# The end of the last tile in a streaming encoder: loads of x on GpSimd's queue, the sample's tokens in four column groups

## The chip, the core and the metric

The kernel runs on one core of a Trainium2 chip. Its engines are TensorE (PE; weight loads are shown as PEld), VectorE (DVE), ScalarE (ACT), GpSimd (POOL) and SyncE (SP, which only issues transfers). The metric is device time in microseconds (us) of one launch; the median of three runs of the kernel before is 2172.12 us.

## What is computed

A two-layer encoder step for 1024 prompt tokens and 32 sample tokens that share all weights. Layer 0 mixes tokens with a spatial-gating unit, layer 1 with pooling windows; each is followed by a channel MLP, each with norms before and behind, and scales that come from a condition vector per group. What matters here is the last line of layer 1:

```python
f = jnp.square(jax.nn.relu(h @ ffn_w_up[i])) @ ffn_w_down[i]
x = x + gt2 * rmsnorm(f, g_norm[i, 3])      # y_prompt (1, 1024, 1024), y_sample (1, 32, 1024)
```

`rmsnorm` divides each token by the root of the mean square of its 1024 channels.

## The kernel before

Activations lie with channels on the 128 partitions (8 blocks of 128 channels, `KB`) and tokens along the columns. There are three tiles of tokens: 384, 384, and 256 prompt tokens with the 32 sample tokens behind them (288 columns). Every float32 matrix product is made of three products of split (high and low) parts. The MLP goes through its 4096 hidden channels in 8 chunks of 512; `ffn_item` does one chunk for one tile: four hidden blocks (`up`), then `down`, which for each of 8 output blocks `d` makes 12 products into one PSUM buffer (three of the kind `pd` rotate) and lets VectorE add them to the accumulator `acc`. Chunks 6 and 7 of layer 1 are done for the first two tiles together, and then for the last tile alone. Apart from a part at the start, the framework's scheduler decides the order on each engine; a helper only feeds it work in the program's order.

For the first two tiles the end (`to_out`, `run`) scales the result, adds x, transposes 32x32 blocks on VectorE (tile `turned`), and writes each channel block with four transfers of 48 KB, three by SP's queue and one by GpSimd's. For the last tile the end is taken apart so that little is left behind the last product:

- In `mix_to_ffn` the x that must be added at the end is written to a scratch tensor `xsd` in HBM.
- In `down`, in chunk 7, block by block: `st.square(d)` squares on ScalarE and sums over blocks on VectorE; `scale_last(d)` (line 1340) scales by a channel's coefficient on ScalarE; `turn_last` (line 1362) turns finished blocks by TensorE, so that tokens lie on partitions.
- `scale_last(0)` also issues the nine loads of x by SP: four of 32 partitions for each of two groups of 128 prompt tokens, one for the 32 sample tokens (`LAST`). Each is 1024 pieces of 128 bytes. VectorE transposes 32x32 blocks of them (line 1355) from `xlast_l` to `xlast_h`.
- `last` (line 1566) turns the rest, sums the squares over partitions by products with ones (`pn_last`, line 1574), takes the reciprocal root with one correction step, and for each of three groups (two of 128 tokens, one of 32) and each half of the channels does one multiply-add on VectorE, `x + r * y`, and one output transfer by SP (line 1602).

`LAST` takes the sample's 32 tokens as the lower rows of a full group of 128 columns, so the turned sample has 32 used partitions and 1024 columns. `room(part, t, name)` gives the buffer that held part `h` or `l` of tile `t`; `xlast_l` and `xlast_h` use those of tile 0.

The framework gives each transfer of SP and ScalarE one of eight landing semaphores, and each of GpSimd one of eight others.

Of the kernel before, what the change touches and what calls it, by code (L numbers as in the profile page):

```python
# [12 lines left out]
ALU = mybir.AluOpType  # L13
AX = mybir.AxisListType

P = 128
D = 1024
KB = D // P
SEQ = 1024
DEC = 32  # L20
# [6 lines left out]
TILES = [(0, 384, 0), (384, 384, 0), (768, 256, DEC)]  # L27
NT = len(TILES)
# [6 lines left out]
def tile_stream_encoder_step(  # L35
# [25 lines left out]
    nc = tc.nc  # L61
    act = nc.scalar.activation
    mm = nc.tensor.matmul
# [33 lines left out]
    ncol = [p + s for _, p, s in TILES]  # L97
# [20 lines left out]
    xd = [dram.tile([P, KB, n], F32, name=f"xd{t}") for t, n in enumerate(ncol)]  # L118
    vd = dram.tile([SEQ + DEC, SGU], F32, name="vd")

    LAST = [(0, 0, P), (P, 0, P), (ncol[-1] - P, P - DEC, DEC)]
    xsd = dram.tile([DEC, KB, P // DEC, ncol[-1]], F32, name="xsd")

    ident = const.tile([P, P], F32, name="ident")
# [21 lines left out]
    def A(t, kb, c0=0, w=None):  # L146
        w = ncol[t] - c0 if w is None else w
        return acc[t][:, kb, HALO + c0 : HALO + c0 + w]


    def room(part, t, name, dtype=F32):
        return work.tile([P, KB, ncol[t]], dtype, tag=f"h{part}{t}", bufs=1, name=name)
# [7 lines left out]
    def ps_ms(name):  # L160
        return psum.tile([P, 512], F32, tag="pm", bufs=3, name=name)
# [7 lines left out]
    def t_st(name):  # L169
        return small.tile([P, 4], F32, tag="st", bufs=6, name=name)  # L170
# [1112 lines left out]
    def ffn_item(p, t, after):  # L1283
        l, c, tiles = passes[p]
        last = t == tiles[-1]
        n = ncol[t]
        hid = []

        def up(j):
            ps = ps_up(f"pf{l}_{c}_{t}_{j}")  # L1290
            products(ps, n, up_terms(("up", p, j), t))
            if last:
                w_finish(("up", p, j))
            r = t_m(f"r{l}_{c}_{t}_{j}")
            act(out=r[:, :n], in_=ps[:, :n], func=AF.Relu)  # L1295
            a, b = t_hid("h", f"fh{l}_{c}_{t}_{j}"), t_hid("l", f"fl{l}_{c}_{t}_{j}")
            act(out=r[:, :n], in_=r[:, :n], func=AF.Square)
            split(a, b, r, n)
            hid.append((a, b))

        def down():
            for d in range(KB):
                ps = ps_dn(f"pg{l}_{c}_{t}_{d}")
                wh, wl = need_w(("dn", p, d // 2))
                terms = []
                for j in range(4):
                    o = j * 256 + (d % 2) * P
                    a, b = hid[j]
                    terms.append((wh[:, o : o + P], wl[:, o : o + P], a[:, :n], b[:, :n]))
                products(ps, n, terms)  # L1310
                accumulate(t, d, ps, c == 0)
                if d == 0 and after is not None:
                    st = Stat(t, f"rf{l}_{t}", l == 0 or t < NT - 1)
                if after is not None:
                    st.square(d)
                    if l == 1 and t == NT - 1:
                        scale_last(d)
                        if d in (2, 4, 6):
                            turn_last(d - 2)
                            turn_last(d - 1)  # L1320
                if last and d % 2 == 1:
                    w_finish(("dn", p, d // 2))
                weave(d % 2)
            if after is not None:
                after(st)

        for j in range(4):
            up(j)
            weave()
            if j == 0:  # L1330
                flush()
        pending.append(down)


    last_ps = {}

    def scale_last(d):
        t = NT - 1
        if d == 0:
            last_ps["x"], last_ps["raw"] = (  # L1340
                room(part, 0, f"xlast_{part}").rearrange("p k n -> p (k n)").rearrange(
                    "p (b d) -> p b d", d=D
                )
                for part in "hl"
            )
            src = xsd.rearrange("c k q n -> c (k q) n")
            for i, (c0, r0, nr) in enumerate(LAST):
                for r1 in range(r0, r0 + nr, DEC):
                    nc.sync.dma_start(
                        last_ps["raw"][r1 : r1 + DEC, i, :].rearrange("p (m n) -> p m n", n=DEC),  # L1350
                        src[:, :, c0 + r1 : c0 + r1 + DEC],
                    )
        if d in (3, 4, 5):
            i, r0, nr = d - 3, LAST[d - 3][1], LAST[d - 3][2]
            nc.vector.transpose(
                out=last_ps["x"][r0 : r0 + nr, i, :], in_=last_ps["raw"][r0 : r0 + nr, i, :]
            )
        for c0, w, v in segs[t]:
            a = A(t, d, c0, w)
            act(out=a, in_=a, func=AF.Copy, scale=coef[:, 1, 3, v, d : d + 1])  # L1360

    def turn_last(d):
        half = d // 4
        for i, (c0, _, _) in enumerate(LAST):
            if d % 4 == 0:
                take = ps_up if half == 0 and i < 2 else (ps_ms if half == 0 or i < 2 else ps_dn)
                last_ps[(i, half)] = take(f"yT{i}_{half}")
            nc.tensor.transpose(
                last_ps[(i, half)][:, (d % 4) * P : (d % 4 + 1) * P], A(NT - 1, d, c0, P), ident
            )  # L1370

    def mix_to_ffn(st, l):
        t = st.t
# [182 lines left out]
    def to_out(st):  # L1556
        t = st.t
        col0, npr, nsm = TILES[t]
        blocks = [
            (c * P, P, y_prompt[0, col0 + c * P : col0 + (c + 1) * P, :]) for c in range(npr // P)  # L1560
        ]
        if nsm:
            blocks.append((npr, nsm, y_sample[0]))

        def last():

            turn_last(KB - 2)
            pn = ps_dn("pn_last")
            nb = len(LAST)
            for k in (0, KB - 1):  # L1570
                if k > 0:
                    turn_last(KB - 1)
                for i, (c0, _, _) in enumerate(LAST):
                    mm(
                        pn[:, 2 * i : 2 * i + 2],
                        st.sq[:, k, c0 : c0 + P],
                        ones[:, 0:2],
                        start=k == 0 and i == 0,
                        stop=k > 0 and i == nb - 1,
                        skip_group_check=True,  # L1580
                    )
            sums = pn[:, : 2 * nb].rearrange("p (b c) -> p b c", c=2)[:, :, 0]
            r, q = (t_st(f"{x}_last")[:, :nb] for x in ("r", "q"))
            act(out=r, in_=sums, func=AF.Abs_reciprocal_sqrt, scale=1.0 / D)
            tt(out=q, in0=r, in1=r, op=ALU.mult)
            stt(out=q, in0=sums, scalar=-0.5 / D, in1=q, op0=ALU.mult, op1=ALU.mult)
            stt(out=r, in0=q, scalar=1.5, in1=r, op0=ALU.add, op1=ALU.mult)
            xt = last_ps["x"]
            dsts = [dst for _, _, dst in blocks]
            for i, (_, r0, nr) in enumerate(LAST):  # L1590
                rows = slice(r0, r0 + nr)
                for half in range(2):
                    d = slice(half * 512, half * 512 + 512)
                    stt(
                        out=xt[rows, i, d],
                        in0=last_ps[(i, half)][rows, :],
                        scalar=r[rows, i : i + 1],
                        in1=xt[rows, i, d],
                        op0=ALU.mult,
                        op1=ALU.add,  # L1600
                    )
                    nc.sync.dma_start(dsts[i][:, d], xt[rows, i, d])
            yield False

        def run():
            need_ada(1, 5)
            if t == NT - 1:
                yield from last()
                return
            yield from residual(st, 1, 3, f"r2_1_{t}", [], store=False, stat=False)  # L1610
            turned = room("h", t, f"turned{t}")
            dst = y_prompt[0, col0 : col0 + npr, :].rearrange(
                "(b i) (k q c) -> q k i b c", i=DEC, q=P // DEC, c=DEC
            )
            for k in range(KB):
                time["dve"] += 0.1 + npr / 930.0
                nc.vector.transpose(out=turned[:, k, :], in_=A(t, k))
                for q in range(P // DEC):
                    (nc.gpsimd if q == 3 else nc.sync).dma_start(
                        dst[q, k],  # L1620
                        turned[DEC * q : DEC * (q + 1), k, :].rearrange("p (b c) -> p b c", c=DEC),
                    )
                yield False

        fillers.append((f"out_{t}", run()))
# [48 lines left out]
```

## Time and profile before

| | |
|---|---|
| median of three runs (lowest to highest) | 2172.12 us (2170.7 to 2173.51) |
| the profiled execution's own time | 2173.74 us |
| its span, from the first to the last recorded instruction | 2171.7 us |
| mean granted TensorE clock | 0.996 |
| TensorE busy | 2145.5 us, 99% |
| VectorE busy | 1431.8 us, 66% |
| ScalarE busy | 971.3 us, 45% |
| GpSimd busy | 13.3 us, 1% |

A row of a timeline gives the start (us from the span's start), the length, engine, line, operation, out<-in, the shape, how many follow each other (xN), and in brackets the idle time before it with what ended it. A row of the chain of waits gives start, length, and engine with tile and line. Groups give busy time, mean ns of one, and idle time. SPq or ACTq is the part of an engine that issues transfers. Helpers hide some lines: L79 is every VectorE helper call, L902 to L904 the three products of a term. A table of stretches lists length, then busy time of PE, PEld, DVE, ACT and POOL with counts, granted clock, share of the DMA engines and GB/s.

### The profile page before, as it was taken

How to read it: one execution, taken by the hardware profiler on the slowest of the kernel's cores; microseconds unless marked ns; L12 is line 12 of the kernel's file. 1: busy time of each engine (PE TensorE's matmuls, PEld its weight loads, DVE VectorE, ACT ScalarE, POOL GpSimd, SP SyncE). 2: the span in 40 equal slices, each digit the busy share in tenths (PEclk: the TensorE clock that was granted, in tenths of full speed). 3: DMA queues.
4: the chain of work that ended last, by engine and by line, in shares of the span. 5: the costliest groups of instructions: out<-in, count | busy, mean ns of one | idle time of the engine just before them, and what ended most of it. 6: DMA issues, size and time to landing. Idle time of an engine off the chain costs nothing.

```text
span 2171.7 us, 33210 instructions
## 1 busy us (share of the span) xinstructions
PE 2145.5 (99%) x13214; PEld 2078.1 (96%) x13214; DVE 1431.8 (66%) x2499; ACT 971.3 (45%) x1643; POOL 13.3 (1%) x30
## 2 busy tenths in 40 slices
PE   7999999999999999999999999999999999999998
PEld 5778899999999999999999999999999999999997
DVE  5688647566879548496747879869675554523377
ACT  4633422234447552323445566666555542313354
POOL 0000000000000000000000000000000000000001
PEclk9999999999999999999999999999999999999999
DMA  8386534343437454243645466565455552302255
GB/s 300 119 269 193 173 93 139 90 148 109 147 96 233 132 155 143 87 140 110 196 129 161 141 189 182 171 191 158 141 161 158 157 155 68 98 20 78 69 139 125
DMA packets 383262, 312.95 MB, mean 144 GB/s; under 512 B 39458, under 2 KB 346346, under 8 KB 383108
## 3 DMA queue, kind: packets, MB, share of 16 engines
q1 hardware_dynamic: 380452, 308.64, 46.8%
q8 instruction: 103, 1.69, 0.3%
q10 hardware_dynamic: 2144, 1.41, 0.2%
q0 software_dynamic: 512, 0.79, 0.1%
q14 instruction: 51, 0.42, 0.1%
HBM read 278.95 MB, written 31.84 MB: 143 GB/s over the span
## 4 chain that ended last, share of the span: by engine, by line
PE 93%; DVE 3%; DMA 2%; ACT 1%; issue 1%; ACTq 0%; DVEq 0%; SPq 0%
PE pg L902 11%; PE pg L903 11%; PE pg L904 11%; PE pf L902 11%; PE pf L904 11%; PE pf L903 11%; PE po L902 3%; PE po L903 3%; PE po L904 3%; PE pu L902 3%; PE pu L904 3%; PE pu L903 3%; PE pv L929 2%; PE pv L930 2%; PE pv L931 2%; PE pp L1532 1%
## 5 line engine op out<-in xcount | busy, mean ns | idle before, releaser
L902 PE MATMUL pg<-fh,wh_dn 128*128 128x384 f32 (+1 forms) x1536 | 495.8, 323 | 0.0
L902 PE MATMUL pf<-hh,wh_up 128*128 128x384 f32 (+1 forms) x1536 | 494.4, 322 | 0.0
L903 PE MATMUL pf<-hl,wh_up 128*128 128x384 f32 (+1 forms) x1536 | 493.1, 321 | 0.0
L904 PE MATMUL pf<-hh,wl_up 128*128 128x384 f32 (+1 forms) x1536 | 492.9, 321 | 0.2 <-DVE wl_up L79 0.2
L903 PE MATMUL pg<-fl,wh_dn 128*128 128x384 f32 (+1 forms) x1536 | 492.6, 321 | 0.4 <-DVE fl L79 0.4
L904 PE MATMUL pg<-fh,wl_dn 128*128 128x384 f32 (+1 forms) x1536 | 492.5, 321 | 0.0
L79 DVE TENSOR_TENSOR wl_up<-raw,wh_up 128x1024 fp32r<-128x1024 f32 x152 | 185.9, 1224 | 165.4 <-ACT wh_up L422 165.4
L902 PEld LDWEIGHTS pg<-fh,wh_dn 128*128 128x128 f32 x1536 | 288.3, 188 | 1.5 <-ACT fh L1121 0.6
L903 PEld LDWEIGHTS pg<-fl,wh_dn 128*128 128x128 f32 x1536 | 288.3, 188 | 1.5 <-DVE fl L79 0.7
L904 PEld LDWEIGHTS pf<-hh,wl_up 128*128 128x128 f32 x1536 | 288.6, 188 | 0.5 <-DVE wl_up L79 0.5
L903 PEld LDWEIGHTS pf<-hl,wh_up 128*128 128x128 f32 x1536 | 288.3, 188 | 0.4
L902 PEld LDWEIGHTS pf<-hh,wh_up 128*128 128x128 f32 x1536 | 288.2, 188 | 0.4
L904 PEld LDWEIGHTS pg<-fh,wl_dn 128*128 128x128 f32 x1536 | 288.3, 188 | 0.0
L422 ACT ACTIVATE wh_up<-raw 128x1024 fp32r<-128x1024 f32 x152 | 161.2, 1060 | 279.9 <-PE pf L903 213.6
L79 DVE TENSOR_TENSOR acc<-acc,pg 128x384 f32<-128x384 f32 (+1 forms) x336 | 174.2, 519 | 146.3 <-PE pg L904 145.7
L422 ACT ACTIVATE wh_dn<-raw 128x1024 fp32r<-128x1024 f32 x152 | 160.8, 1059 | 202.9 <-PE pg L903 170.6
L79 DVE TENSOR_TENSOR wl_dn<-raw,wh_dn 128x1024 fp32r<-128x1024 f32 x152 | 186.0, 1224 | 82.4 <-ACT wh_dn L422 82.2
L79 DVE SCALAR_TENSOR_TENSOR aa<-raw,csil,aa 128x512 f32<-128x512 f32 (+1 forms) x364 | 203.5, 623 | 8.0 <-DMA raw<-in_w_ada_dram 7.9
L1295 ACT ACTIVATE r<-pf 128x384 f32<-128x384 f32 (+1 forms) x192 | 86.6, 451 | 201.9 <-PE pf L904 199.2
L79 DVE TENSOR_TENSOR fl<-r,fh 128x384 fp32r<-128x384 f32 (+1 forms) x192 | 100.3, 523 | 85.4 <-ACT fh L1121 84.3
L902 PE MATMUL pu<-hh,wh_u 128*128 128x384 f32 (+1 forms) x384 | 125.8, 328 | 0.0
L902 PE MATMUL po<-ush,wh_o 128*128 128x384 f32 (+1 forms) x384 | 123.5, 322 | 0.0
(263 smaller groups left out, 2927.2 us busy)
## 6 DMA issues: line engine op xcount, KB each, us to landing
raw<-in_ffn_w_up_dram SPq DMA_DIRECT2D x152, 512.0 KB, 3.9
raw<-in_ffn_w_down_dram SPq DMA_DIRECT2D x152, 512.0 KB, 3.5
raw<-in_w_ada_dram SPq DMA_DIRECT2D x96, 512.0 KB, 4.3
raw<-in_sgu_w_in_dram SPq DMA_DIRECT2D x40, 512.0 KB, 4.4
xd<-acc SPq DMA_DIRECT2D x8, 1536.0 KB, 7.8
raw<-in_sgu_w_out_dram SPq DMA_DIRECT2D x24, 512.0 KB, 4.0
xo_r<-xd SPq DMA_DIRECT2D x32, 384.0 KB, 3.4
vd<-vt SPq DMA_DIRECT2D x32, 256.0 KB, 4.5
```

Source lines behind the costliest of these rows:

```text
L79: return op(out, *args, **kw)
L422: act(out=wh, in_=r, func=AF.Copy)
L902: mm(ps[:, :n], wh, rh, start=i == 0, stop=False)
L903: mm(ps[:, :n], wh, rl, start=False, stop=False)
L904: mm(ps[:, :n], wl, rh, start=False, stop=i == last)
L929: mm(ps[:m, :], a_h, wh[:, o : o + 512], start=k == 0, stop=False)
L930: mm(ps[:m, :], a_h, wl[:, o : o + 512], start=False, stop=False)
L931: mm(ps[:m, :], a_l, wh[:, o : o + 512], start=False, stop=k == KB - 1)
L1295: act(out=r[:, :n], in_=ps[:, :n], func=AF.Relu)
L1532: mm(ps[:, :n], wg[:, k, e * P : (e + 1) * P], A(t, 2 * g + k), start=k == 0, stop=k == 1)
```

## The change

Loading x moves from `scale_last(0)` into `load_last`, called when the last tile's chunk 6 starts, on GpSimd's queue: 16 transfers of 512 pieces and four of 256. The 32 sample tokens are laid out with four groups of 256 channels on four groups of 32 partitions: their x (four loads), their turned blocks (a plain product with the identity whose result goes to a quarter of the partitions, `tile_position`), their sums of squares (four narrow products), one transpose, one multiply-add of 128x256, and four output transfers by ScalarE's queue. The eighth block's scaling moves to VectorE. The last turn stands behind both rounds of sums. The turned second halves of prompt and sample use the buffers of the kind `pm`.

```diff
-    LAST = [(0, 0, P), (P, 0, P), (ncol[-1] - P, P - DEC, DEC)]
+    LAST = (0, P)
...
+        if l == 1 and c == 6 and t == NT - 1:
+            load_last()
         for j in range(4):
             up(j)
...
+    def load_last():
+        raw = room("l", 0, "xlast_l").rearrange("p k n -> p (k n)")
+        src = xsd.rearrange("c k q n -> c (k q) n")
+        parts = [
+            (i * D + 512 * half, 16, r1, slice(16 * half, 16 * half + 16), c0 + r1)
+            for i, c0 in enumerate(LAST)
+            for half in range(2)
+            for r1 in range(0, P, DEC)
+        ]
+        parts += [
+            (2 * D, 8, DEC * g, slice(8 * g, 8 * g + 8), TILES[-1][1]) for g in range(P // DEC)
+        ]
+        for at, m, r1, ms, n0 in parts:
+            nc.gpsimd.dma_start(
+                raw[r1 : r1 + DEC, at : at + m * DEC].rearrange("p (m n) -> p m n", n=DEC),
+                src[:, ms, n0 : n0 + DEC],
+            )
...
     def scale_last(d):
...
-        if d in (3, 4, 5):
-            i, r0, nr = d - 3, LAST[d - 3][1], LAST[d - 3][2]
-            nc.vector.transpose(
-                out=last_ps["x"][r0 : r0 + nr, i, :], in_=last_ps["raw"][r0 : r0 + nr, i, :]
-            )
+        if d in (1, 2, 3):
+            c = slice((d - 1) * D, min(d * D, 2 * D + 256))
+            nc.vector.transpose(out=last_ps["x"][:, c], in_=last_ps["raw"][:, c])
+        if d == KB - 1:
+            for c0, w, v in segs[t]:
+                a = A(t, d, c0, w)
+                ts(a, a, coef[:, 1, 3, v, d : d + 1], None, op0=ALU.mult)
+            return
...
     def turn_last(d):
...
+        if d == 0:
+            last_ps["s"] = ps_ms("yTs")
+        q = d // 2 * DEC
+        mm(
+            last_ps["s"][q : q + DEC, d % 2 * P : d % 2 * P + P],
+            A(NT - 1, d, TILES[-1][1], DEC),
+            ident,
+            start=True,
+            stop=True,
+            tile_position=(0, q),
+            skip_group_check=True,
+        )
...
             for k in (0, KB - 1):
-                if k > 0:
-                    turn_last(KB - 1)
-                for i, (c0, _, _) in enumerate(LAST):
+                for i in range(2):
                     mm(
                         pn[:, 2 * i : 2 * i + 2],
-                        st.sq[:, k, c0 : c0 + P],
+                        st.sq[:, k, cols[i]],
...
+                for q in range(0, P, DEC):
+                    mm(
+                        pn[q : q + DEC, 4:6],
+                        st.sq[:, k, npr:],
+                        ones[:, 0:2],
+                        start=False,
+                        stop=k > 0,
+                        tile_position=(0, q),
+                        skip_group_check=True,
+                    )
+            turn_last(KB - 1)
...
-                    nc.sync.dma_start(dsts[i][:, d], xt[rows, i, d])
+                    nc.sync.dma_start(blocks[i][2][:, d], x)
+            x = xt[:, 2 * D : 2 * D + 256]
+            stt(
+                out=x,
+                in0=last_ps["s"][:, :256],
+                scalar=r[:, 2:3],
+                in1=x,
+                op0=ALU.mult,
+                op1=ALU.add,
+            )
+            for g in range(P // DEC):
+                nc.scalar.dma_start(
+                    blocks[2][2][:, g * 256 : (g + 1) * 256], x[DEC * g : DEC * (g + 1), :]
+                )
```

More of the change, by code (lines that the diff above doesn't have):

```diff
@@ L1335, in tile_stream_encoder_step @@
     last_ps = {}
+    def load_last():
[15 more added lines that the diff above has]
+            )
+        last_ps["raw"] = raw
     def scale_last(d):
@@ L1339, in scale_last @@
         if d == 0:
-            last_ps["x"], last_ps["raw"] = (
-                room(part, 0, f"xlast_{part}").rearrange("p k n -> p (k n)").rearrange(
-                    "p (b d) -> p b d", d=D
-                )
[L1344 to L1352, printed above, removed]
-        if d in (3, 4, 5):
-            i, r0, nr = d - 3, LAST[d - 3][1], LAST[d - 3][2]
-            nc.vector.transpose(
-                out=last_ps["x"][r0 : r0 + nr, i, :], in_=last_ps["raw"][r0 : r0 + nr, i, :]
-            )
+            last_ps["x"] = room("h", 0, "xlast_h").rearrange("p k n -> p (k n)")
+        if d in (1, 2, 3):
[6 more added lines that the diff above has]
+            return
         for c0, w, v in segs[t]:
@@ L1363, in turn_last @@
         half = d // 4
-        for i, (c0, _, _) in enumerate(LAST):
+        for i, c0 in enumerate(LAST):
             if d % 4 == 0:
-                take = ps_up if half == 0 and i < 2 else (ps_ms if half == 0 or i < 2 else ps_dn)
-                last_ps[(i, half)] = take(f"yT{i}_{half}")
+                last_ps[(i, half)] = (ps_up if half == 0 else ps_ms)(f"yT{i}_{half}")
             nc.tensor.transpose(
@@ L1568, in last @@
             pn = ps_dn("pn_last")
-            nb = len(LAST)
+            cols = [slice(c0, c0 + P) for c0 in LAST]
             for k in (0, KB - 1):
-                if k > 0:
-                    turn_last(KB - 1)
-                for i, (c0, _, _) in enumerate(LAST):
+                for i in range(2):
                     mm(
                         pn[:, 2 * i : 2 * i + 2],
-                        st.sq[:, k, c0 : c0 + P],
+                        st.sq[:, k, cols[i]],
                         ones[:, 0:2],
                         start=k == 0 and i == 0,
-                        stop=k > 0 and i == nb - 1,
+                        stop=False,
                         skip_group_check=True,
                     )
-            sums = pn[:, : 2 * nb].rearrange("p (b c) -> p b c", c=2)[:, :, 0]
-            r, q = (t_st(f"{x}_last")[:, :nb] for x in ("r", "q"))
+                for q in range(0, P, DEC):
[9 more added lines that the diff above has]
+            turn_last(KB - 1)
+            sums = pn[:, :6].rearrange("p (b c) -> p b c", c=2)[:, :, 0]
+            r, q = (t_st(f"{x}_last")[:, :3] for x in ("r", "q"))
             act(out=r, in_=sums, func=AF.Abs_reciprocal_sqrt, scale=1.0 / D)
@@ L1588, in last @@
             xt = last_ps["x"]
-            dsts = [dst for _, _, dst in blocks]
-            for i, (_, r0, nr) in enumerate(LAST):
-                rows = slice(r0, r0 + nr)
+            for i in range(2):
                 for half in range(2):
                     d = slice(half * 512, half * 512 + 512)
+                    x = xt[:, i * D + half * 512 : i * D + half * 512 + 512]
                     stt(
[L1595 to L1598, printed above, removed]
+                        out=x,
+                        in0=last_ps[(i, half)],
+                        scalar=r[:, i : i + 1],
+                        in1=x,
                         op0=ALU.mult,
@@ L1601, in last @@
                     )
-                    nc.sync.dma_start(dsts[i][:, d], xt[rows, i, d])
+                    nc.sync.dma_start(blocks[i][2][:, d], x)
+            x = xt[:, 2 * D : 2 * D + 256]
+            stt(
+                out=x,
+                in0=last_ps["s"][:, :256],
+                scalar=r[:, 2:3],
+                in1=x,
+                op0=ALU.mult,
[5 more added lines that the diff above has]
+                )
             yield False
```

## The prediction

> **What bounds the kernel now.** I read the page first: its totals and the chain of waits.
>
> ```profile
> span 2171.7 us, 33210 instructions
> PE 2145.5 (99%) x13214; PEld 2078.1 (96%) x13214; DVE 1431.8 (66%) x2499; ACT 971.3 (45%) x1643; POOL 13.3 (1%) x30
> PE 93%; DVE 3%; DMA 2%; ACT 1%; issue 1%; ACTq 0%; DVEq 0%; SPq 0%
> ```
>
> TensorE sets the time nearly everywhere; the edit concerns the last stretch, so next the chain in order of time, from the last product on.
>
> ```profile
> 2158.91 0.15 PE pg L904
> ...
> 2160.93 0.18 ACT r_last L1584
> ```
>
> The last product ends at 2159.06; add, square, sums of squares and reciprocal root follow one after the other. The timeline of VectorE shows what comes then.
>
> ```profile
> 2161.14 0.16 DVE L79 TENSOR_TENSOR q_last<-r_last 128x3 f32<-128x3 f32 x1 [1.60 <-ACT r_last L1584]
> 2161.41 0.16 DVE L79 SCALAR_TENSOR_TENSOR q_last<-pn_last,q_last 128x3 f32<-128x3 f32 x1
> 2161.60 0.16 DVE L79 SCALAR_TENSOR_TENSOR r_last<-q_last,r_last 128x3 f32<-128x3 f32 x1
> 2161.80 1.41 DVE L79 SCALAR_TENSOR_TENSOR xlast_h<-yT,r_last,xlast_h 128x512 f32<-128x512 f32 x2
> 2163.13 1.23 DVE L1355 STREAM_TRANSPOSE xlast_h<-xlast_l 128x1024 f32<-128x1024 f32 x1
> 2164.40 1.41 DVE L79 SCALAR_TENSOR_TENSOR xlast_h<-yT,r_last,xlast_h 128x512 f32<-128x512 f32 x2
> 2165.84 1.24 DVE L1355 STREAM_TRANSPOSE xlast_h<-xlast_l 32x1024 f32<-32x1024 f32 x1
> 2167.11 1.44 DVE L79 SCALAR_TENSOR_TENSOR xlast_h<-yT,r_last,xlast_h 32x512 f32<-32x512 f32 x2
> ```
>
> From 2161.80 to 2168.55 VectorE alone is the path: six multiply-adds, with two transposes of x between them. The 32-row forms last as long as the 128-row ones. The view of the tile xlast_h, SP's waits and the DMA list give the rest:
>
> ```profile
> L1602 SPq DMA_DIRECT2D out_dram<-xlast_h x6: 332/340/357, 2162.6 to 2168.6; - x6
> DMA to landing us min/median/max: 1.7/2.0/2.1
> SPq L1602 <- DVE xlast_h L79: 8.5, 6, 4.6
> out_dram<-xlast_h SPq DMA_DIRECT2D x4, 256.0 KB, 2.0
> out_dram<-xlast_h SPq DMA_DIRECT2D x2, 64.0 KB, 1.7
> ```
>
> The last output is issued at 2168.6, lands 1.7 later, and 1.4 us of closing work end the span. SP stands still at a wait (4.6 us for one) with all that is queued behind it.
>
> **The change part by part.** Times are those of the profiled execution (span 2171.7, its own time 2173.74). The median of the runs shown, 2172.12, is 1.6 below that execution, so the change in us is added to the median.
>
> *Off VectorE's path.* The built order puts all three transposes of x (1024, 1024 and 256 columns) ahead of the last products. After the root remain four multiply-adds of 128x512, each (2163.13 - 2161.80)/2 = 0.66, and one of 128x256, about 0.42 (half of 0.66 and a start). That is 3.06 in place of 6.75: 3.7 us less.
>
> *Loads of x.* SP loses nine issues, none of them on the path. GpSimd gets 16 issues of 512 pieces and 4 of 256 instead, where the trace has 384:
>
> ```profile
> L1619 POOL DMA_DIRECT2D out_dram<-turned x16: 615/615/748, 2110.2 to 2154.2; - x16
> 2078.34 0.62 DVE L79 SCALAR_TENSOR_TENSOR sm_rf<-sq_rf,eps,sc_rf 128x384 fp32r<-128x384 f32 x1 [0.68 <-ACT sc_rf L780]
> 2110.16 0.75 POOL L1619 DMA_DIRECT2D out_dram<-turned  x1 [1521.63 <-DVE turned L1617]
> ```
>
> By pieces that is 16 x 0.82 + 4 x 0.41 = 15 us, from 2079 (when sm_rf has freed the buffer) to about 2095; what is queued behind it starts at 2110. I cost it at nothing; GpSimd's idle time covers it, and 15 us more would have to go wrong first.
>
> *Transposes earlier, last scaling on VectorE.* Both go where VectorE has room:
>
> ```profile
> 2149.00:2154.00 5.00, 5.00 (x41) 4.87 (x40) 5.00 (x10) 3.52 (x9) 0.43 (x1) 1.00 0.46 77
> 2154.00:2159.00 5.00, 5.00 (x42) 5.00 (x41) 2.95 (x7) 3.50 (x9) 0.81 (x2) 1.00 0.65 110
> ```
>
> The columns after the length are PE, PEld, DVE, ACT and POOL. VectorE is full until 2154 and then has 2.05 us free; the 1.6 us of transposes fit into that. While they run, the adds that give TensorE its product buffers come about 0.5 to 1.5 us later; three buffers rotate, so TensorE has a whole block of twelve products (12 x 0.13 us) in hand. Cost 0, up to 0.5. The scaling (about 0.5) fits into VectorE's 1.60 us of idling before q_last.
>
> *Sums ahead of the last turn.* In the built order of the kernel before, the six sums already stand ahead of the last three turns. This part moves nothing.
>
> *Sample's turns in column groups.* Per channel block a full-width transpose of 0.11 us (2152.71 to 2152.96 with two more, below) goes, and a 32-column float32 product streaming 128 columns at a column position comes. Float32 products are two records each. Their streaming cost, and a nearest case of column positions:
>
> ```profile
> 318.31 0.61 PE L1213 MATMUL psp<-wr,vl 128*128 128x128 f32 x4
> 318.75 0.31 PE L1221 MATMUL psp<-wr,vl 128*128 128x32 f32 x2
> 877.41 0.33 PE L903 MATMUL pf<-hl,wh_up 128*128 128x384 f32 x1
> 877.59 0.34 PE L904 MATMUL pf<-hh,wl_up 128*128 128x384 f32 x1
> 877.86 0.26 PE L459 MATMUL ada<-sums,squares 128*32 128x16 f32 x8
> 878.05 0.40 PE L902 MATMUL pf<-hh,wh_up 128*128 128x288 f32 x1
> 878.29 0.29 PE L903 MATMUL pf<-hl,wh_up 128*128 128x288 f32 x1
> 878.42 0.29 PE L904 MATMUL pf<-hh,wl_up 128*128 128x288 f32 x1
> 2152.71 0.49 PE L1368 MATMUL yT<-ident,acc 128*128 128x128 f32 x3
> 2152.96 0.38 PE L902 MATMUL pg<-fh,wh_dn 128*128 128x288 f32 x1
> ```
>
> Four records in 0.44 us are 0.11 each. Lower end: two records for one transpose, +0.11 a block; less is excluded, since two passes stream as many columns as the one did. Upper end from L459: after 877.59 the next start is due at 877.76 (0.17 apart) and the one after it 0.13 later, at 877.89; it came at 878.29. Eight tiny products at column positions delay the stream by 0.40; with two streams of 128 columns and less one transpose, +0.40 + 0.22 - 0.11 = +0.51. The nearest row is L459, whose 0.40 has its own short streams in it: I take +0.40 a block. Six blocks lie ahead of the last product, where TensorE has no idle time: +2.4 (0.7 to 3.1).
>
> After the last product: a seventh block, +0.40; both rounds of sums lose one full-width product of two records (4 x 0.11 = 0.45) and gain four narrow ones, 0.40 a round; and TensorE's idling goes:
>
> ```profile
> 2160.06 0.74 PEld L1574 LDWEIGHTS pn_last<-ones,sq_rf 128*128 128x128 f32 x6 [0.21 <-ACT sq_rf L750]
> ```
>
> So +0.40 + 0.80 - 0.45 - 0.21 = +0.54 (0 to 0.9).
>
> *Sample's outputs on ACT's queue: the part that decides.* In the built program each DMA of SP or ACT takes the next of eight landing semaphores and waits until the DMA that had it before has landed. They are dealt in the scheduler's order, and it dealt four to ACT's outputs ahead of SP's last ten DMAs. The rows, with waits:
>
> ```
> ACT 1555 out_1_dram<-xlast_h 32x256 [waits DMAHW3,DVE]
> ACT 1556 out_1_dram<-xlast_h 32x256 [waits DMAHW5]
> SP 682 out_0_dram<-turned1 32x12x32 [waits DMAHW2]
> SP 683 out_0_dram<-turned1 32x12x32 [waits DMAHW3,DVE]
> ...
> SP 688 out_0_dram<-turned1 32x12x32 [waits DMAHW0]
> SP 689 out_0_dram<-xlast_h 128x512 [waits DMAHW1,DVE]
> ...
> SP 692 out_0_dram<-xlast_h 128x512 [waits DMAHW4,DVE]
> ```
>
> The value that SP 683 waits for on semaphore 3 is reached only when ACT 1555 has landed, and that one waits for the very last multiply-add. Behind SP 683 stand five more pieces of the middle tile and all four 256 KB outputs of the last tile. In the trace before, SP had issued those pieces by 2157.9, under the products; here they start after everything. Their pace, and the transfers' own:
>
> ```profile
> 2151.74 6.18 SPq L1619 DMA_DIRECT2D out_dram<-turned  x12
> 2162.00:2165.00 3.00, 0.00 (x0) 0.00 (x0) 2.96 (x4) 0.00 (x0) 0.00 (x0) 0.64 0.45 175
> ```
>
> Twelve in 6.18 are 0.515 each. In 2162 to 2165 two transfers of 256 KB took a share of 0.45 of the DMA engines: 0.675 us each at full share, more than their issue (0.35, about 0.41 apart). Four in a row land 2.0 + 3 x 0.675 = 4.03 after the first issue (lower end 2.0 + 3 x 0.41 = 3.23). [...]
>
> *The sum.* Root at 2160.93 + 2.4 + 0.54 = 2163.87. First multiply-add 0.87 later, 2164.74; after five (3.06) 2167.80. ACT's first output lands 1.7 later: 2169.5. Six pieces, 3.09: 2172.6. The four outputs, 4.03: 2176.6. Closing, 1.4: **2178.0, or +6.3 us**. On the median: 2178.4. Lower ends together: +0.7 and 0 at TensorE, 3.23 at the outputs give 2174.9, +3.2 (2175.3). Upper ends: 3.1 and 0.9, a landing of 2.1, and one issue that takes 1.7 as SP's longest did (315/468/1712 ns over the 48 issues of that line) give about +8.9 (2181.0).
>
> **The rivals.**
>
> *A: SP is held, but column positions cost only their streaming.* +0.11 a block, sums cheaper: +3.2 to +4, 2175.3 to 2176.1. For it: within L459's group the records start a few ns apart, so part of its 0.40 may be what follows 384-column products only. [...]
>
> *B: the change does what it says, and is not slower.* If SP's last ten DMAs go out in time (ACT's landings not needed for them), the path after the last multiply-add is four ACT issues, 3 x 0.40, a landing of 1.7 and 1.4 of closing: 2167.80 + 4.3 = 2172.1, +0.4; with A's cheap blocks 2169.9, -1.8. It decides if semaphore 3 fills before 2165. For it: the 3.7 us off VectorE are real. Against it: the wait stands in the program, and SP's own waits show that it stops in order. Even then it is within 0.2%.
>
> *C: worse.* Pieces of 128 bytes and 256 KB outputs compete, or GpSimd's 20 loads delay weights around 2080 to 2095: beyond +8.9, 2181 to 2184. Against the second: the code holds up to eight split weights ahead of their use.
>
> **How the numbers follow.** Forecast 0.72, A 0.16, B 0.07, C 0.05. 0.2% is 4.3 us, about what a measurement of this kernel can tell from no change; slower by more needs over 2176.5. The forecast's spread reaches below that in about one case in ten, A mostly, B nearly always, and a gain of 4.3 us has hardly any way to come about. So slower 0.71, same 0.26, faster 0.03. The range runs from 2173.5 (between A and B) to 2181.0 (upper ends).
>
> **What would show it.** On SP's timeline: an idle stretch of over 10 us at the middle tile's pieces, ended by the landing of ACT's first output, then ten issues in a row at the very end. In VectorE's timeline five multiply-adds without a transpose between them. On TensorE each yTs group 0.3 to 0.5 longer than before, and the last product ending near 2161.5. It would be wrong if SP issues those pieces before the last product ends, or if the last product still ends near 2159.7.

## The result and the profile after

The changed kernel takes 2186.75 us (median of six runs, 2185.88 to 2188.41), the kernel before 2171.5 us beside it (2169.45 to 2173.51). The ratio is 1.0071, with a 95% interval of 1.0058 to 1.0083: 15.25 us slower, where 6.3 were forecast. The profiled execution took 2185.98 us, its span 2183.8.

Up to the last 110 us both programs issue the same work in nearly the same order, yet one execution reaches a given instruction some us earlier or later than another. So the two traces are compared from an instruction near the end that both have, the first turn `yT`. Its row in the timeline of TensorE, before:

```profile
2148.89 0.82 PE L1368 MATMUL yT<-ident,acc 128*128 128x128 f32 x6
...
2152.58 0.29 PE L904 MATMUL pg<-fh,wl_dn 128*128 128x288 f32 x1
...
2153.17 0.29 PE L903 MATMUL pg<-fl,wh_dn 128*128 128x288 f32 x1
```

and the same stretch after:

```profile
2144.50 0.30 PE L904 MATMUL pg<-fh,wl_dn 128*128 128x288 f32 x1
2144.63 0.38 PE L1379 MATMUL yT<-ident,acc 128*128 128x128 f32 x2
2144.94 0.41 PE L1385 MATMUL yTs<-ident,acc 128*32 128x128 f32 x2
...
2145.52 0.29 PE L903 MATMUL pg<-fl,wh_dn 128*128 128x288 f32 x1
...
2155.26 0.69 PE L1379 MATMUL yT<-ident,acc 128*128 128x128 f32 x2 [8.53 <-ACT acc L1372]
...
2160.05 0.38 PE L1379 MATMUL yT<-ident,acc 128*128 128x128 f32 x2
```

From the first turn to the end of the span it is 2171.7 - 2148.89 = 22.8 us before and 2183.8 - 2144.63 = 39.2 us after, 16.4 more. This "time from the first turn" is used below beside the medians, because what the executions differ in ahead of it drops out. Two things are to be seen in the rows. A block with a column group holds the stream of products from 2144.50 to 2145.52, 1.02 us, where a block before took from 2152.58 to 2153.17, 0.59: 0.43 more. And TensorE stands still for 8.53 us ahead of the second block's turn. The timeline of VectorE says why:

```profile
2152.60 1.25 DVE L1364 STREAM_TRANSPOSE xlast_h<-xlast_l 128x1024 f32<-128x1024 f32 x1 [9.95 <-DMA out_dram<-turned]
2153.77 0.41 DVE L79 TENSOR_TENSOR acc<-acc,pg 128x288 f32<-128x288 f32 x1
...
2170.62 2.73 DVE L79 SCALAR_TENSOR_TENSOR xlast_h<-yT,r_last,xlast_h 128x512 f32<-128x512 f32 x4
2173.26 0.48 DVE L79 SCALAR_TENSOR_TENSOR xlast_h<-yTs,r_last,xlast_h 128x256 f32<-128x256 f32 x1
```

The first transpose of x stands ahead of the add of block 1, and waits 9.95 us. It does not wait for x, whose last load landed at 2140.57 by the trace: it waits for an output of `turned`, the first tile's turned result, whose buffer `xlast_h` takes over. A quarter of those outputs are on GpSimd's queue, and they are the late ones. Its timeline is:

```profile
2075.35 0.78 POOL L1352 DMA_DIRECT2D xlast_l<-xsd  x1 [1490.46 <-DVE sm_rf L79]
2078.14 0.66 POOL L1352 DMA_DIRECT2D xlast_l<-xsd  x1 [2.01 <-issue]
2082.74 0.65 POOL L1352 DMA_DIRECT2D xlast_l<-xsd  x1 [3.94 <-issue]
...
2137.18 1.74 POOL L1352 DMA_DIRECT2D xlast_l<-xsd  x3 [1.43 <-issue]
2139.77 0.61 POOL L1663 DMA_DIRECT2D out_dram<-turned  x1 [0.85 <-DVE turned L1661]
...
2150.32 1.25 POOL L1663 DMA_DIRECT2D out_dram<-turned  x2 [1.04 <-issue]
```

The loads of 512 pieces go out one at a time, 3 to 6 us apart (50.7 us of waiting at 16 issues, which no other engine ends): by the trace's landings, each goes out 0.30 us after the one ahead of it has landed. Only the last ones, of 256 pieces, follow each other directly. The first piece of `turned` goes out at 2139.77; before it was at 2110.16. The eighth, the last that the first tile has on this queue, goes out at 2150.32 and lands at 2152.33; the transpose starts at 2152.60. The prediction let the loads end at about 2095.

The end, in a timeline of all engines:

```profile
2173.77 1.77 ACTq L1644 DMA_DIRECT2D out_dram<-xlast_h  x4
2175.37 3.21 SPq L1663 DMA_DIRECT2D out_dram<-turned  x6
2178.69 1.89 SPq L1633 DMA_DIRECT2D out_dram<-xlast_h  x4
```

and in SP's waits:

```profile
SPq L1663 <- DMA out_dram<-xlast_h: 28.2, 1, 28.2
```

SP stands for 28.2 us until ScalarE's first output has landed, and then sends its last ten transfers after everything else.

### The profile page after: what moved, and what is told of

Same layout as the page of the kernel before. It is cut to its first block, busy times and chain, and to the rows that moved or that the text cites. A ratio compares the mean times of both kernels' runs of the same rounds, so it can differ in the third digit from the quotient of the medians.

```text
span 2183.8 us, 33266 instructions
## 1 busy us (share of the span) xinstructions
PE 2146.1 (98%) x13234; PEld 2076.9 (95%) x13234; DVE 1430.7 (66%) x2500; ACT 970.2 (44%) x1641; POOL 26.1 (1%) x50
## 4 chain that ended last, share of the span: by engine, by line
PE 90%; issue 3%; DVE 3%; DMA 2%; ACT 1%; POOL 1%; DVEq 0%; SPq 0%; ACTq 0%; POOLq 0%
PE pg L902 11%; PE pg L904 10%; PE pg L903 10%; PE pf L902 10%; PE pf L904 10%; PE pf L903 10%; PE po L902 3%; PE po L903 3%; PE po L904 3%; PE pu L902 3%; PE pu L904 2%; PE pu L903 2%; PE pv L929 2%; PE pv L930 2%; PE pv L931 2%
```

## The experiments

The theory after this reading: of the 16.4 us, two stalls are nearly all. Loads that run one at a time on GpSimd keep `turned` from leaving its buffer, and VectorE waits for that buffer in front of an add that TensorE needs; and SP's hold at the end. The rivals: the loads themselves, by landing late or by what they take from the DMA engines; and the transfers at the end, whoever issues them.

**Sample's outputs on SP.**

```diff
-                nc.scalar.dma_start(
+                nc.sync.dma_start(
                     blocks[2][2][:, g * 256 : (g + 1) * 256], x[DEC * g : DEC * (g + 1), :]
```

> Only the sample's four outputs go back from ACT's queue to SP's. Theory: SP was held 28.2 us because landing semaphores that its last ten transfers need were filled only by ACT's outputs. Without that, the four 256 KB outputs leave one by one behind their multiply-adds, the sample's four outputs follow 0.4 us apart, the last lands about 4.3 us after the last multiply-add has ended, and closing work of 1.1 us makes the span end; from the last multiply-add to the end 10.05 us become about 4.3, so 5.8 us less than the changed kernel, about +9.4 us against the kernel before. The idle 9.95 us of VectorE ahead of the first transpose of x stays. Rival (the transfers themselves are the bound at the end, whoever issues them): the end stays within 1.5 us of the changed kernel's.

2181.19 us; against the kernel before 1.0042 (1.0027 to 1.0057), +9.2 us. VectorE:

```profile
2149.60 1.25 DVE L1364 STREAM_TRANSPOSE xlast_h<-xlast_l 128x1024 f32<-128x1024 f32 x1 [6.37 <-DMA out_dram<-turned]
...
2170.02 0.48 DVE L79 SCALAR_TENSOR_TENSOR xlast_h<-yTs,r_last,xlast_h 128x256 f32<-128x256 f32 x1
```

From the last multiply-add (2170.50) to the end of the span (2174.6) it is 4.1 us, after the change 2183.8 - 2173.74 = 10.1: the hold cost 6.0, as expected, and the other stall stays (6.4 us in the profiled execution, which took 2176.75 us and is the fastest of four; the others took 2180.9 to 2181.8). The rival on the transfers falls.

**Loads cut to 256 pieces, still on GpSimd, outputs as in the changed kernel.**

```diff
-            (i * D + 512 * half, 16, r1, slice(16 * half, 16 * half + 16), c0 + r1)
+            (i * D + 256 * half, 8, r1, slice(8 * half, 8 * half + 8), c0 + r1)
             for i, c0 in enumerate(LAST)
-            for half in range(2)
+            for half in range(4)
```

> The changed kernel with each of the 16 loads of 512 pieces cut into two of 256 pieces, still on GpSimd: the same bytes and the same pieces in 36 transfers. [...] Rival (the rate is set by pieces or bytes, not by how many transfers are on their way): the loads end at 2139 or later, with more fixed cost, the stall stays or grows: +15 us or more.

2178.33 us, 1.003 (1.0019 to 1.0042), +6.4 us, where about +5 was forecast; the forecast took three of 256 pieces on their way at a time, as the last three loads of the changed kernel go out (`x3` at 2137.18). GpSimd's and VectorE's timelines:

```profile
2078.75 1.87 POOL L1352 DMA_DIRECT2D xlast_l<-xsd  x3 [1491.21 <-DVE sm_rf L79]
2081.24 1.79 POOL L1352 DMA_DIRECT2D xlast_l<-xsd  x3 [0.62 <-issue]
...
2123.25 0.62 POOL L1663 DMA_DIRECT2D out_dram<-turned  x1 [0.95 <-DVE acc L79]
```

```profile
2146.35 1.25 DVE L1364 STREAM_TRANSPOSE xlast_h<-xlast_l 128x1024 f32<-128x1024 f32 x1 [0.31 <-DMA out_dram<-turned]
2147.52 0.42 DVE L79 TENSOR_TENSOR acc<-acc,pg 128x288 f32<-128x288 f32 x1
```

Now three loads leave together, the last is issued by 2122 instead of 2139, and 9.95 us of waiting become 0.31. The same bytes in the same pieces over the same queue cost nothing when they leave the queue in time: it was not the amount that counted, but how few of the large transfers the queue has on their way. The order of the instructions on TensorE, VectorE, ScalarE and SP is the same as in the changed kernel.

**Both sets of transfers on SP.** In the kernel with the sample's outputs on SP, line 1352 becomes `nc.sync.dma_start`.

> The sample's outputs and the 20 loads of x both on SP's queue. Theory: GpSimd's loads run one at a time and keep turned0's eight pieces from going out, so the transposes into that buffer wait; with the loads elsewhere the wait of 9.95 us, TensorE's starving behind it and the lower clock that follows are gone: about 10 us less than with the outputs alone moved, so -0.6 us against the kernel before (-2 to +1.5). The column groups still cost 0.43 us each. Rival (the loads themselves, by what they take from the DMA engines or by landing late, hold the transpose): an idle stretch of several us ahead of the first transpose stays, and the time is +4 or more against the kernel before.

2185.96 us, 1.0067 (1.005 to 1.0084), +14 us: a miss by the theory's number. But no wait for `turned` is left; VectorE shows something else:

```profile
2159.26 2.70 DVE L1364 STREAM_TRANSPOSE xlast_h<-xlast_l 128x1024 f32<-128x1024 f32 x3 [0.30 <-issue]
2161.88 1.18 DVE L79 TENSOR_TENSOR wl_dn<-raw,wh_dn 128x1024 fp32r<-128x1024 f32 x1
2162.98 2.69 DVE L79 TENSOR_TENSOR acc<-acc,xo_r 128x768 f32<-128x768 f32 x3
```

With 20 issues of about 0.5 us more on SP the scheduler builds another order. The middle tile's reloads of x go behind the first tile's outputs, and its residual (`acc<-acc,xo_r`) and turning then stand in VectorE's queue ahead of the last blocks; the weight split that a product needs stands behind three transposes. This kernel tests the scheduler's order more than the wait, and does not decide between the theories: its transposes stand at 2159.26, later than their wait ended in the changed kernel (2152.60).

**Sample's outputs on SP, and all pieces of `turned` too; loads of 512 pieces stay on GpSimd.**

```diff
-                    (nc.gpsimd if q == 3 else nc.sync).dma_start(
+                    nc.sync.dma_start(
```

> The sample's outputs on SP's queue, and the pieces of the turned tiles that GpSimd issued go to SP too; the 20 loads of x stay on GpSimd. Theory: nothing is queued behind the loads any more, so the transpose waits only for the loads themselves, which landed at 2140.6, 12 us before it ran: the stall is gone although the loads are as slow as before; -0.6 us against the kernel before (-2 to +2; SP has 16 issues more of 0.5 us). Rival (loads themselves): the stall stays, +6 to +10.

2177.51 us, 1.0026 (1.0016 to 1.0037), +5.6 us: better than +9.2, but not -0.6. GpSimd's waits, VectorE, TensorE and the stretches around them (columns as in the prediction):

```profile
POOL xlast_l L1352 <- issue: 51.8, 16, 5.0
```

```profile
2154.90 2.70 DVE L1364 STREAM_TRANSPOSE xlast_h<-xlast_l 128x1024 f32<-128x1024 f32 x3 [0.31 <-issue]
2157.52 1.19 DVE L79 TENSOR_TENSOR wl_dn<-raw,wh_dn 128x1024 fp32r<-128x1024 f32 x1
```

```profile
2154.70 0.44 PE L1379 MATMUL yT<-ident,acc 128*128 128x128 f32 x2 [1.01 <-ACT acc L1372]
...
2155.85 0.40 PE L902 MATMUL pg<-fh,wh_dn 128*128 128x288 f32 x1 [0.38 <-ACT wh_dn L422]
...
2158.76 0.41 PE L904 MATMUL pg<-fh,wl_dn 128*128 128x288 f32 x1 [2.11 <-DVE wl_dn L79]
```

```profile
2158.00:2160.00 2.00, 1.24 (x6) 1.24 (x7) 1.97 (x3) 0.00 (x0) 0.00 (x0) 0.75 0.00 0
2160.00:2162.00 2.00, 2.00 (x10) 2.00 (x10) 1.10 (x3) 0.14 (x1) 0.00 (x0) 0.50 0.29 49
```

The loads are as slow as ever, and the transposes wait for nothing. By itself this says less than it seems, because the scheduler has put the transposes at 2154.90 here, later than the end of their wait in the changed kernel (2152.60). That loads landing late hold them is ruled out by the changed kernel's own trace, where the last load had landed 12 us before the wait ended; that the loads hold them by what they take from the DMA engines is ruled out by the kernel with 256 pieces, which moves the same bytes in the same pieces. What is left of the time here is again the order. Three transposes in a row stand ahead of the split of weights `wl_dn`; TensorE stands for 3.5 us within 5, its granted clock falls to 0.50, and its products run at about half pace (10 in 2 us) after the wait is over.

**Both repairs with the order kept: 256 pieces on GpSimd, sample's outputs on SP.** The first two diffs together; TensorE's order is that of the changed kernel, VectorE's too but for one small instruction long before the end.

> Both repairs together, with the order of all other work as in the changed kernel: loads of 256 pieces on GpSimd, sample's outputs on SP. Theory: the two costs are separate and add up. The loads of 256 pieces alone measured +6.4 us against the kernel before, and the end from the last multiply-add fell from 10.0 us to 4.1 us when the outputs moved: 6.4 - 5.9 = +0.5 us against the kernel before (-1 to +2). What is left is the gain of 3.7 us on VectorE's path, eaten by the column groups (2.6 us) and by four sample outputs in a row on SP (about 1 us). Rival (the two hide each other, or the stall is only moved): +3 or more.

2171.06 us beside 2171.42 for the kernel before, 1.0 (0.9991 to 1.0009). TensorE's first turns, and VectorE's end:

```profile
2146.12 0.38 PE L1379 MATMUL yT<-ident,acc 128*128 128x128 f32 x2
...
2148.07 0.38 PE L1379 MATMUL yT<-ident,acc 128*128 128x128 f32 x2
...
2151.06 0.38 PE L1379 MATMUL yT<-ident,acc 128*128 128x128 f32 x2
```

```profile
2160.96 0.16 DVE L79 TENSOR_TENSOR q_last<-r_last 128x3 f32<-128x3 f32 x1 [0.74 <-ACT r_last L1616]
...
2164.27 0.48 DVE L79 SCALAR_TENSOR_TENSOR xlast_h<-yTs,r_last,xlast_h 128x256 f32<-128x256 f32 x1
```

This settles the sizes. From the first turn to the second it is 1.95 us here and 10.63 after the change: 8.7 of standing still. From the second to the third it is 2.99 here and 4.79 there: 1.8 of a lowered clock. The hold is the difference between this kernel and the one with 256 pieces alone, in time from the first turn 28.6 - 22.8 = 5.8. Together 16.3 of the 16.4 us; what is left of the change is worth 0.0.

**The sample as before, loads and transposes early.** The kernel just shown, with `LAST`, `turn_last`, the sums and the multiply-adds of the kernel before.

> As the run with both repairs, but the sample's tokens stay in the layout of the kernel before: full-width transposes, 32-row multiply-adds, two outputs; loads of x early in 256 pieces and transposes of x ahead of the last products stay. Theory: the last product ends where it ended in the kernel before (the column groups' 0.43 us each are gone: -2.6), the multiply-adds take 4.1 us instead of 3.1 (+1.0), the last output is issued 0.4 instead of 1.2 us after its multiply-add (-0.5 or so): about 2 us less than with both repairs, -1.6 us against the kernel before (-3 to 0). Rival (column groups cost little, and the last product was late for what VectorE has taken over): the last product stays 2 us late and the time is +1 or more against the kernel before.

2169.55 beside 2171.42 us, 0.9992 (0.9983 to 1.0001); from the first turn 20.6 us, 2.2 less than before. The two transposes that have left VectorE's path behind the root were 1.23 and 1.24 us. Against the kernel with both repairs, the sample's new layout as a whole costs 22.8 - 20.6 = 2.2 us (1.5 by the medians): more on TensorE than the shorter multiply-adds save.

**Column groups in batches.** In `turn_last` the sample's products wait until four blocks can go together, then three, then one; the x loads and the outputs follow the changed places, and the narrow sums of both rounds stand together behind the wide ones.

```diff
+        for e in {5: range(4), 6: range(4, 7), 7: (7,)}.get(d, ()):
+            q = e % 4 * DEC
             mm(
-                last_ps["s"][q : q + DEC, d % 2 * P : d % 2 * P + P],
-                A(NT - 1, d, TILES[-1][1], DEC),
+                last_ps["s"][q : q + DEC, e // 4 * P : e // 4 * P + P],
+                A(NT - 1, e, TILES[-1][1], DEC),
```

> As the run with both repairs, but the sample's turns in column groups are done in batches: four channel blocks together, then three, then the last one, so that TensorE goes into and out of the narrow form twice ahead of the last products instead of six times. Theory (the price is paid for each going in and out, not for each product): the batch of four takes about 0.43 + 3 x 0.2 us or less, the last product ends about 1.2 us earlier than with both repairs, and the time is about -0.8 us against the kernel before (-2 to +1). Rival (each narrow product has its own price): the last product ends where it does with both repairs, and the time is the same as there.

2168.77 beside 2171.42 us, 0.999 (0.9981 to 0.9999); from the first turn 21.1 us. TensorE:

```profile
2152.53 0.30 PE L904 MATMUL pg<-fh,wl_dn 128*128 128x288 f32 x1
...
2152.98 0.42 PE L1392 MATMUL yTs<-ident,acc 128*32 128x128 f32 x8
...
2153.57 0.29 PE L903 MATMUL pg<-fl,wh_dn 128*128 128x288 f32 x1
```

With four narrow products the stretch from 2152.53 to 2153.57 takes 1.04 us; with one it took 1.02. So the price is paid once for each visit to the narrow form, and four products at four positions cost no more than one. How much of it is going in and out, and how much is four products that run side by side, this run does not separate. The gain of 1.7 us from the first turn is more than the 1.2 us forecast for the last product.

**Fewer issues at the end.** From the batched kernel, once with the sample's four outputs as one transfer of 128 KB on SP, once with its multiply-add first and its outputs on GpSimd.

> As the run with batched groups, with the sample's 128 KB going out in one transfer on SP instead of four. In the batched run the four issues stood 0.64 us apart behind the last multiply-add, and the last landed 3.9 us after it, with 1.1 us of closing. Theory (the last issue sets the end): one issue of 0.4 to 0.6 us and a landing of about 2 us, so 1.7 us less: -4.3 us against the kernel before (-5.5 to -2.5). Rival (a transfer of 256 pieces in one issue lands as late as four of 64): the same -2.6 as the batched run.

> As the run with batched groups, with the sample's multiply-add ahead of the other four and its four outputs on GpSimd's queue, which has its own landing semaphores and nothing behind them. Theory: they go out under the other multiply-adds; the last on the path is a 256 KB output, 2.0 us from issue to landing, and 1.1 us of closing: about 3.3 us from the last multiply-add to the end instead of 5.0, -4.2 us against the kernel before (-5.5 to -2.5). Rival (GpSimd's own closing work comes late when its last transfers are late): the span ends later, -2 or worse.

2171.05 us, 0.9998 (0.999 to 1.0007), and 2169.74 us, 0.9989 (0.998 to 0.9998), each beside 2172.23: neither gives the 1.7 us. From the first turn they take 20.9 and 20.7 us against 21.1. So three versions lie about 0.1% below the kernel before; for two of them the interval only just leaves out 1 (upper ends 0.9999 and 0.9998), at most the hint of a gain. In the first the issues are saved, but the one transfer is slow: from 2166.1 to 2167.4, with little else on its way, the DMA engines are busy to between 0.2 and 0.3 and move 80 to 86 GB/s. In the second the lists of transfers show something else:

```profile
out_dram<-xlast_h SPq DMA_DIRECT2D x4, 256.0 KB, 3.1
out_dram<-xlast_h POOLq DMA_DIRECT2D x4, 32.0 KB, 2.8
```

The 256 KB outputs land 3.1 us after their issue instead of 2.0. What holds them up, the small outputs beside them or something else, was not shown.

**How many loads are on their way.** Both repairs, the loads cut to 128 pieces.

> As the run with both repairs, with the loads of x cut again, into 72 of 128 pieces, on GpSimd. What is measured is how many are on their way at once: one of 512 pieces, three of 256 in the runs so far. [...] Rival (a fixed number of three transfers on their way, whatever their size): every fourth load waits for a landing, and the 72 loads take about 70 us or more.

A single run: 2175.49 beside 2169.8 us, but 22.7 us from the first turn (2150.29 to 2173.0), as both repairs: it had lost its time before the first turn, and one run does not say whether by the loads or by chance. GpSimd:

```profile
2081.01 6.64 POOL L1354 DMA_DIRECT2D xlast_l<-xsd  x12 [1491.84 <-DVE sm_rf L79]
...
2115.02 2.26 POOL L1354 DMA_DIRECT2D xlast_l<-xsd  x4 [0.59 <-issue]
```

Twelve leave in a row, 0.55 us each, and 72 loads take 43 us: no fixed number of three. The load at 2115.02 waited with seven on their way, the first of which landed at 2114.71. So one of 512 pieces, three of 256 and seven of 128; 384 pieces, in the rows of `turned`, two. A limit of 896 to 1023 pieces on their way fits all four; what sets it was not shown. Another buffer for the transposed x was not tried.

## Why the prediction was wrong

- *Five multiply-adds, 3.06 us.* From 2170.62 to 2173.74, 3.12. Right.
- *"By pieces that is 16 x 0.82 + 4 x 0.41 = 15 us ... I cost it at nothing; GpSimd's idle time covers it."* This step failed, and nearly the whole error is here. The issues took 0.65 us each, less than assumed; what the step left out is the landing of the load ahead that each had to wait for, 50.7 us in all, so the loads were issued until 2139 instead of about 2095. And its reserve of 15 us was measured to the next work in the queue, without asking who waits for that work. In place of nothing the step cost 8.7 us of standing still and 1.8 us of a lowered clock. The sign stood in the trace before, in GpSimd's timeline:

```profile
2119.23 1.33 POOL L1619 DMA_DIRECT2D out_dram<-turned  x2 [2.13 <-issue]
2122.84 1.23 POOL L1619 DMA_DIRECT2D out_dram<-turned  x2 [2.27 <-issue]
```

  Transfers of 384 pieces go out in twos, with 2.2 us between the pairs that no other engine ends. Read as a limit on the pieces on their way, two of 384 and not three, this gives one or two at a time for 512 pieces. With one at a time the loads take 16 landings of 3 us, the order of what came; with two, about half of that. So the trace before gave the warning, but not the size.
- *Transposes earlier, "cost 0, up to 0.5".* Their own time cost nothing (0.31 us of idling in the kernel with 256 pieces). But the step weighed only their length, not the wait that stands in front of them in VectorE's queue, with the adds behind it: 9.95 us, where it counted 12 products of 0.13 us in TensorE's hand.
- *Column groups, +2.4 before the last product and +0.54 behind it.* From the first turn to `q_last` it was 2161.14 - 2148.89 = 12.25 us before and 14.84 with both repairs: +2.59 for a forecast of +2.94. The price of a block, 0.40, was measured at 0.43; ahead of the last product it came to +2.4, and behind it to +0.2 instead of +0.54. In the batched kernel four products pay one price (a stretch of 1.04 us, against 1.02 with one product); what part of it is going in and out of the narrow form was not shown.
- *SP's hold.* Right in place and size: six pieces in 3.21 (forecast 3.09), from the last multiply-add to the end 10.1 us (10.2).
- *The sum.* The kernel with 256 pieces is the change with this one step mended, and it came out at +6.4 us, where +6.3 had been forecast. Its interval is about +4 to +9, and from the first turn it is 28.6 - 22.8 = +5.8, so the terms are borne out, but the tenth of a us is luck. Of the rivals, A and B fell: a block cost 0.43 and not 0.11, and SP was held. C's time (2181 to 2184) lies nearest the measured one, but not by its mechanism: it had GpSimd's loads delay weights, and TensorE's only wait from 2070 to the end is the 8.53 us, which no weight ended.

## What to carry to other kernels

Before moving transfers to another queue, look in the trace for how many of that size the queue has on their way at once (here one of 512 pieces, with 3.3 us from issue to landing and 0.65 for the issue), and multiply landings, not issues; then follow the work behind them in the queue to the engine that waits for its buffer. A wait put into a queue costs what stands behind it (here 9.95 us on VectorE became 8.53 on TensorE), so look at which add or weight split comes next. The column groups paid once for each visit to the narrow form (0.43 us here, for one product as for four), so products of such a form are worth batching; transfers split between two issuing engines may share landing semaphores, as ScalarE's and SP's do here, and then one queue holds the other (SP stood for 28.2 us).

## What the runs showed of the hardware

In the changed kernel TensorE's granted clock falls from 1.00 to 0.50 while it stands still for 8.53 us, and stays there after work is back. By stretches:

```profile
2146.00:2155.00 9.00, 0.73 (x6) 0.50 (x4) 2.40 (x3) 0.75 (x2) 3.75 (x7) 0.67 0.24 46
2155.00:2158.00 3.00, 2.74 (x10) 2.03 (x11) 3.00 (x5) 0.70 (x3) 1.80 (x3) 0.50 0.16 33
```

The last product ahead of the wait ends at 2146.73. The clock is 1.00 from 2148 to 2149 and 0.50 from 2149 to 2150, and it is still 0.50 for at least 3 us after work is back, which cost the 1.8 us above. It falls some 2.3 us after the last product in the changed kernel, and in the kernel with all pieces of `turned` on SP to the same 0.50 although no single pause was over 2.11 us. And eight records of narrow products at four column positions are done in 0.42 us in the batched kernel, two records at one position in 0.41 in the changed one, while a visit to that form, with the way in and out, costs 0.43 us more than the full-width transpose in its place.
